# Splitting weights by two transfers on GpSimd's queue, one that rounds and one that accumulates, instead of a load, a cast and a subtraction

## The chip, the cores and the metric

The kernel runs on one core of a Trainium2 chip. The metric is the device time of one execution in microseconds, as the median of several runs. The profile is of one execution; its times are counted from its first instruction.

## What is computed

Two blocks of layers, two layers each, on a sequence of 512 tokens with 1024 features, all in 32-bit floats. The first block has a Fourier mix, windowed attention and attention to a memory in front of a gated feed-forward; the second has a feed-forward, a mixer of three branches and another feed-forward:

```python
for l in range(DEPTH):                       # first block
    h = _rmsnorm(x, g_pre_mix[l]); z = h @ w_in[l]
    y = concat(rmsnorm(fourier), rmsnorm(window attention), rmsnorm(memory attention)) @ w_out[l]
    x = x + _rmsnorm(y, g_post_mix[l])
    gate, up = jnp.split(_rmsnorm(x, g_pre_ffn[l]) @ w_ffn_in[l], 2, axis=-1)
    x = x + _rmsnorm((jax.nn.silu(gate) * up) @ w_ffn_out[l], g_post_ffn[l])
for l in range(DEPTH):                       # second block
    x = x + 0.5 * swiglu(rms_norm(x, ffn1_norm[l]), ffn1_w1[l], ffn1_w2[l])
    x = x + hybrid_mixer(rms_norm(x, mix_norm[l]), ...)   # linear recurrence, attention, depthwise convolution of 31 taps
    x = x + 0.5 * swiglu(rms_norm(x, ffn2_norm[l]), ffn2_w1[l], ffn2_w2[l])
```

## The kernel before

Activations lie with features on the 128 partitions and the 512 tokens along the free dimension, in tiles of 128 x 512 floats ("s", from one pool of 95 slots of 2 KB for each partition). A product of 32-bit floats is made of three matmuls in a shorter float format, fp32r: each operand is split into a rounded part h and a remainder l = value - h, and `mm3` adds wh x al, wl x ah and wh x ah in PSUM. Every weight is used for one pass over the 512 tokens, so all weights stream through once, 12 matmuls for a half tile of 128 x 512 weights.

A weight's way before the change (`wload`, `wsmall`): SP issues a load of up to 1024 columns into "raw" (a pool "wp" of three tiles of 4 KB for each partition); for each half of 512 columns `split` then makes h by a cast (`Plan.copy`, on ScalarE or VectorE) and l by a subtraction (`Plan.tt`, on VectorE or GpSimd), both into slots. Activations are split in the same way, from slots or from PSUM. GpSimd also takes other sums and products of the program through `Plan.tt`, as long as no operand is in PSUM. The only transfers on its queue are the 32 loads of the Fourier tables (`fourier`), from 32-bit floats in HBM into fp32r slots; they round on the way.

The order of all instructions is made ahead by `Plan.schedule`: it simulates the five engines with the prices of `Plan.price`, and among the instructions that are ready and whose tiles find room gives each engine the one that TensorE needs first, up to 120 us ahead of TensorE (AHEAD). An instruction with several possible engines goes to the one that would end it first. The result is a fixed program: each engine works through its own list in order and waits by semaphores. Since every instruction is issued in one helper, `Plan.issue`, all have its line in the profile, L647 before and L646 after the change; groups are told apart by engine, operation and tiles.

In the second block, `mixer` runs `mla` (attention, with the projections of the two other branches as `filler` between), then `dwconv` for four tiles, each a chain of 30 scalar_tensor_tensor instructions on VectorE, one for each tap, with 482 to 511 columns; branches 1 and 0, whose matmuls don't need the convolution; `conv_norm`, which does; and branch 2.

## Time and profile before

| what | value |
|---|---|
| time, median of 3 runs (lowest to highest) | 3626.53 us (3625.71 to 3627.09) |
| span of the profiled execution | 3625.2 us |
| TensorE busy with matmuls | 3460.9 us, 95% |
| VectorE busy | 2558.2 us, 71% |
| ScalarE busy | 1008.3 us, 28% |
| GpSimd busy | 735.2 us, 20% |
| read from HBM | 319.91 MB, 90 GB/s over the span |
| share of the 16 DMA engines | 27.2% for SP's queue, 0.5% for GpSimd's |

Busy time of an engine is the time in which it works on an instruction, and waits inside an instruction count as work. The idle time of an engine is put down to what ended it. The table by stretch (rows 3 below) gives each engine's busy time in that stretch, the number of its instructions in brackets, TensorE's granted clock as a share of full speed, the mean share of the DMA engines and what they moved.

### The profile page before, as it was taken

To read this page: it belongs to the slowest core of one execution; us is meant where nothing else is said; L and a number is where in the kernel's file an instruction comes from. 1 tells how busy PE (TensorE), PEld (TensorE's weight loads), DVE (VectorE), ACT (ScalarE), POOL (GpSimd) and SP (SyncE) were. 2 spreads that over 40 slices of the span, in tenths; PEclk is the share of its full clock that TensorE was granted. 3 is DMA by queue.
4 is the path that set the end of the run, shared out by engine and by line. 5 is a ranking of instruction groups with operands and counts; after the bars stand their busy time and mean duration, and the time that the engine had idled before them with its cause. 6 is when DMAs were issued, how large, how long until landed. Compare 5 with 4: busy or idle time off the path is not lost.

```text
span 3625.2 us, 42725 instructions
## 1 busy us (share of the span) xinstructions
PE 3460.9 (95%) x16280; PEld 2874.0 (79%) x16280; DVE 2558.2 (71%) x4377; ACT 1008.3 (28%) x1944; POOL 735.2 (20%) x582
## 2 busy tenths in 40 slices
PE   7999999989999999999995999999999999599998
PEld 6788888778888888887784888888888878488887
DVE  8987545888553865479999765566556999975553
ACT  5632112453110311037523211021102662321110
POOL 4341003443000400013434000000001243510000
PEclk8999999999999999999997999999999999899999
DMA  4223232232223232331222422332233122242231
GB/s 143 81 66 111 82 102 73 81 99 76 82 94 98 81 109 84 103 118 55 93 72 86 139 76 80 108 121 78 80 112 133 42 72 93 81 138 83 80 104 50
DMA packets 105406, 331.61 MB, mean 91 GB/s; under 512 B 12272, under 2 KB 21232, under 8 KB 105200
## 3 DMA queue, kind: packets, MB, share of 16 engines
q1 hardware_dynamic: 100592, 324.64, 27.2%
q0 software_dynamic: 4608, 4.23, 0.5%
q8 instruction: 128, 2.10, 0.2%
q14 instruction: 78, 0.64, 0.1%
HBM read 319.91 MB, written 6.29 MB: 90 GB/s over the span
## 4 chain that ended last, share of the span: by engine, by line
PE 76%; DVE 21%; issue 2%; ACT 1%; DMA 0%; POOL 0%; SPq 0%; DVEq 0%; ACTq 0%; POOLq 0%
PE ps L647 76%; DVE s L647 20%; ACT s L647 1%; DVE nb L647 0%; DMA s<-in_x 0%; DVE mx L647 0%; DMA raw<-in_a_in 0%; DVE sp L647 0%; POOL rinv L647 0%; SPq L647 0%; DVE rc L647 0%; POOL s L647 0%; DVE sums L647 0%; DVE rms L647 0%; DVEq L647 0%
## 5 line engine op out<-in xcount | busy, mean ns | idle before, releaser
L647 PE MATMUL ps<-s 128*128 128x512 f32 (+3 forms) x15706 | 3399.8, 378 | 44.9 <-DVE s L647 36.0
L647 PEld LDWEIGHTS ps<-s 128*128 128x128 f32 (+1 forms) x15706 | 2804.5, 189 | 609.1 <-DVE s L647 50.0
L647 DVE TENSOR_TENSOR s<-ps,s 128x512 f32<-128x512 f32 (+5 forms) x642 | 394.8, 635 | 515.6 <-PE ps L647 512.2
L647 DVE TENSOR_TENSOR s<-raw,s 128x512 fp32r<-128x512 f32 (+1 forms) x918 | 640.1, 719 | 23.4 <-ACT s L647 5.5
L647 POOL TENSOR_TENSOR s<-s 128x512 f32<-128x512 f32 (+2 forms) x277 | 335.1, 1219 | 1526.6 <-DVE s L647 893.2
L647 POOL TENSOR_TENSOR s<-raw,s 128x512 fp32r<-128x512 f32 (+1 forms) x250 | 366.6, 1480 | 1177.0 <-ACT s L647 534.7
L647 ACT ACTIVATE s<-s 128x512 f32<-128x512 f32 (+1 forms) x325 | 182.6, 579 | 1074.6 <-DVE s L647 1041.1
L647 DVE TENSOR_TENSOR s<-s 128x512 f32<-128x512 f32 (+3 forms) x573 | 423.9, 746 | 60.5 <-ACT s L647 35.9
L647 ACT CAST s<-raw 128x512 fp32r<-128x512 f32 (+1 forms) x564 | 326.4, 606 | 434.9 <-DMA raw<-in_b 181.1
L647 DVE SCALAR_TENSOR_TENSOR s<-s,vecs 128x256 fp32r<-128x256 f32 (+25 forms) x446 | 386.2, 897 | 2.8
L647 DVE CAST s<-raw 128x512 fp32r<-128x512 f32 (+1 forms) x604 | 277.9, 466 | 21.2 <-DMA raw<-in_b 10.9
L647 ACT ACTIVATE s<-s,vecs 128x512 f32<-128x512 f32 (+2 forms) x211 | 134.5, 654 | 389.5 <-DVE s L647 354.2
L647 DVE SCALAR_TENSOR_TENSOR s<-ps,s 128x512 f32<-128x512 f32 (+1 forms) x33 | 22.2, 674 | 236.4 <-PE ps L647 236.4
L647 ACT CAST s<-s 128x512 fp32r<-128x512 f32 (+1 forms) x97 | 58.6, 609 | 235.4 <-DVE s L647 183.2
L647 ACT ACT_TABLE_LOAD x68 | 87.2, 1283 | 54.0 <-DVE s L647 52.2
L647 DVE CAST s<-s 128x512 fp32r<-128x512 f32 (+2 forms) x167 | 87.3, 523 | 14.4 <-POOL s L647 10.6
L647 PE MATMUL ps<-ident,s 128*128 128x128 f32 x392 | 65.9, 293 | 31.0 <-DVE s L647 29.0
L647 ACT ACTIVATE s<-ps 128x512 f32<-128x512 f32 (+1 forms) x40 | 21.3, 533 | 235.6 <-PE ps L647 235.5
L647 DVE RECIPROCAL s<-s 128x128 f32<-128x128 f32 (+1 forms) x48 | 83.3, 1742 | 4.2 <-ACT s L647 4.0
L647 PE MATMUL ps<-s,onesr 128*128 128x512 f32 x36 | 13.0, 444 | 76.5 <-DVE s L647 42.3
L647 PEld LDWEIGHTS ps<-ident,s 128*128 128x128 f32 x392 | 49.3, 149 | 46.2 <-DVE s L647 34.2
L647 ACT ACTIVATE s<-s,nb 128x256 f32<-128x256 f32 (+3 forms) x128 | 70.6, 553 | 37.5 <-DVE nb L647 37.3
(61 smaller groups left out, 701.1 us busy)
## 6 DMA issues: line engine op xcount, KB each, us to landing
raw<-in_b SPq DMA_DIRECT2D x240, 512.0 KB, 3.3
raw<-in_a_f SPq DMA_DIRECT2D x120, 512.0 KB, 3.3
raw<-in_b_in SPq DMA_DIRECT2D x92, 512.0 KB, 3.2
raw<-in_b SPq DMA_DIRECT2D x32, 384.0 KB, 3.6
raw<-in_a_in SPq DMA_DIRECT2D x19, 512.0 KB, 4.2
raw<-in_a_out SPq DMA_DIRECT2D x16, 512.0 KB, 3.2
raw<-in_b_out SPq DMA_DIRECT2D x16, 512.0 KB, 3.2
raw<-in_a_f SPq DMA_DIRECT2D x16, 384.0 KB, 3.6
```

Source lines behind the costliest of these rows:

```text
L647: getattr(getattr(nc, op.eng), op.fn)(*[real(v) for v in op.args], **{k: real(v) for k, v in op.kw.items()})
```

## The change

A half tile of weights no longer passes through "raw". GpSimd's queue issues a transfer from HBM into h that rounds to fp32r; `Plan.scale` makes l = -h (on ScalarE or VectorE); and GpSimd's queue issues a second transfer of the same weights that adds them onto l. Both transfers read the weights from HBM. "wp" is gone, and the pool of slots has 100 instead of 95. `Plan.tt` no longer offers GpSimd. The planner's price for issuing a transfer there is 0.6 instead of 1.0 us, and it now books these transfers on the DMA engines, an accumulating one with double its bytes. The rest of the difference is removed comments.

```diff
     def tt(self, out, in0, in1, op):
-        kw = dict(out=out, in0=in0, in1=in1, op=op)
-        ways = [("vector", "tensor_tensor", (), kw)]
-        if not any(v.tile.psum for v in (out, in0, in1)):
-            ways.append(("gpsimd", "tensor_tensor", (), kw))
-        self.record(ways)
+        self.record([("vector", "tensor_tensor", (), dict(out=out, in0=in0, in1=in1, op=op))])
...
         if fn == "dma_start":
-            return 1.0
+            return 0.6
...
                         elif op.fn == "dma_start":
-                            op.end = now + 4.0
+                            n = int(np.prod(op.kw["out"].shape[1:]))
+                            passes = 2 if "accum_op" in op.kw else 1
+                            state["dma"] = max(state["dma"], now + 1.0) + passes * 128 * n * 4 / 330e3
+                            op.end = state["dma"] + 1.6
...
-    NSLOT = 95
-    RBUFS = 3
+    NSLOT = 100
...
-    def wload(self, src):
+    def halves(self, src):
         nc = self.nc
         n = src.shape[1]
-        raw = nc.tile("wp", "raw", [128, 8, 128], F32, self.RBUFS)[:, :n]
-        for c in (0, 4) if self.fresh else (0,):
-            e = c + 4 if self.fresh else n
-            nc.sync.dma_start(out=raw[:, c:e], in_=src[:, c:e])
-        self.fresh = False
-        hs, ls = [], []
-        for c in range(0, n, 4):
-            e = min(c + 4, n)
-            h, l = (self.t(F32R)[:, :128 * (e - c)].rearrange("p (k c) -> p k c", c=128) for _ in range(2))
-            self.split(raw[:, c:e], h, l)
-            hs.append(h)
-            ls.append(l)
-        return Weights(hs), Weights(ls)
+        h, l = (self.t(F32R)[:, :128 * n].rearrange("p (k c) -> p k c", c=128) for _ in range(2))
+        nc.gpsimd.dma_start(out=h, in_=src)
+        nc.scale(l, h, -1.0)
+        nc.gpsimd.dma_start(out=l, in_=src, accum_op=ALU.add)
+        return h, l
+
+    def wload(self, src):
+        n = src.shape[1]
+        parts = [self.halves(src[:, c:min(c + 4, n)]) for c in range(0, n, 4)]
+        return Weights([h for h, _ in parts]), Weights([l for _, l in parts])
 
     def wsmall(self, src):
-        n = src.shape[1]
-        raw, wh, wl = (self.t(dt)[:, :128 * n].rearrange("p (k c) -> p k c", c=128) for dt in (F32, F32R, F32R))
-        self.nc.sync.dma_start(out=raw, in_=src)
-        self.split(raw, wh, wl)
-        return wh, wl
+        return self.halves(src)
...
-        pools = {k: es.enter_context(tc.tile_pool(name=k, bufs=1)) for k in ("const", "slots", "wp", "sm")}
+        pools = {k: es.enter_context(tc.tile_pool(name=k, bufs=1)) for k in ("const", "slots", "sm")}
```

In the program after the change there are 1196 half tiles (most of 128 x 512, some of 256 or 384 columns) and so 2392 transfers of weights on GpSimd's queue, each of which waits for the completion of the one eight places before it, as transfers on SP's queue do in both programs. The scalings by -1 fall to VectorE 805 times and to ScalarE 391 times.

VectorE in the first mixer of the second block, at the end of the first tile of dwconv (its taps go down to 482 columns); "raw" rows are subtractions for weights, "ps" rows read PSUM. Before:

```order
L647 TENSOR_TENSOR s_16348<-ps_16304,s_14006 128x512
L647 SCALAR_TENSOR_TENSOR s_15970<-s_14364,vecs_115,s_15970 128x484
L647 SCALAR_TENSOR_TENSOR s_16020<-s_14429,vecs_115,s_16020 128x503
L647 TENSOR_TENSOR s_16362<-raw_16287,s_16322 128x512
L647 SCALAR_TENSOR_TENSOR s_15970<-s_14364,vecs_115,s_15970 128x483
L647 TENSOR_TENSOR s_16370<-raw_16287,s_16343 128x512
L647 SCALAR_TENSOR_TENSOR s_15970<-s_14364,vecs_115,s_15970 128x482
```

The same place after:

```order
L646 TENSOR_TENSOR s_16257<-ps_16278,s_16257 128x512
L646 SCALAR_TENSOR_TENSOR s_15978<-s_14376,vecs_109,s_15978 128x484
L646 SCALAR_TENSOR_TENSOR s_15978<-s_14376,vecs_109,s_15978 128x483
L646 SCALAR_TENSOR_TENSOR s_15987<-s_14415,vecs_109,s_15987 128x498
L646 SCALAR_TENSOR_TENSOR s_15978<-s_14376,vecs_109,s_15978 128x482
L646 SCALAR_TENSOR_TENSOR s_15987<-s_14415,vecs_109,s_15987 128x497
```

The subtractions for weights between the taps are gone, and the scalings of the weights that are loaded meanwhile stand on ScalarE's list.

GpSimd in the same mixer, during dwconv. Before:

```order
L647 TENSOR_TENSOR s_16533<-raw_16430,s_16509 128x512
L647 TENSOR_TENSOR s_15911<-s_15911,s_16480 128x512
L647 TENSOR_TENSOR s_16562<-raw_16472,s_16555 128x512
L647 TENSOR_TENSOR s_15964<-s_15964,s_16520 128x512
L647 TENSOR_TENSOR s_16603<-raw_16535,s_16586 128x512
L647 TENSOR_TENSOR s_16649<-s_15970,s_16020 128x512
```

After (s_16274 and s_16312 are remainders, each the second transfer for a half tile):

```order
L646 DMA s_16253<-in_b_lo0 128x512
L646 DMA s_16262<-in_b_in0 128x512
L646 DMA s_16274<-in_b_in0 128x512
L646 DMA s_16295<-in_b_in0 128x512
L646 DMA s_16316<-in_b_in0 128x512
L646 DMA s_16312<-in_b_in0 128x512
```

The subtractions are replaced by transfers, two for each half tile, and the sums that merge the branches (s_15911, s_15964) and that begin conv_norm (s_16649) have gone to VectorE.

GpSimd at the start of the program, after the change, from the 13th transfer on (s_73 and s_101 are the first two rounded halves of the first tile of weights, s_123 and s_186 their remainders):

```order
L646 DMA s_158<-in_a_in0 128x512
L646 DMA s_160<-in_a_in0 128x512
L646 DMA s_166<-in_a_in0 128x512
L646 DMA s_172<-in_a_in0 128x512
L646 DMA s_178<-in_a_in0 128x512
L646 DMA s_182<-in_a_in0 128x512
L646 DMA s_188<-in_a_in0 128x512
L646 DMA s_186<-in_a_in0 128x512
```

The remainder s_123 is the 7th transfer on this list and s_186 the 20th; before, these weights came on SP's list in two of its first eight transfers, between the tiles of x.

## Rows read from the trace of the kernel before

**Rows 1.** The page's first part: busy us, share, instructions of an engine.

```profile
PE 3460.9 (95%) x16280; PEld 2874.0 (79%) x16280; DVE 2558.2 (71%) x4377; ACT 1008.3 (28%) x1944; POOL 735.2 (20%) x582
```

**Rows 2.** What TensorE waited for: us in total, times, longest us.

```profile
PE ps L647 <- DVE s L647: 111.3, 71, 35.3
PE ps L647 <- POOL s L647: 34.2, 1, 34.2
```

**Rows 3.** Stretch: length, PE, PEld, DVE, ACT, POOL busy; PEclk, DMA share, GB/s.

```profile
0.00:243.00 243.00, 208.41 (x1122) 172.88 (x1122) 217.21 (x425) 129.81 (x304) 108.46 (x100) 0.92 0.31 99
243.00:604.00 361.00, 360.71 (x1737) 305.10 (x1738) 207.25 (x345) 65.50 (x124) 44.63 (x40) 1.00 0.28 91
604.00:846.00 242.00, 215.21 (x1277) 179.89 (x1277) 218.19 (x422) 124.87 (x309) 124.22 (x121) 0.96 0.25 79
846.00:1192.00 346.00, 345.74 (x1603) 290.10 (x1602) 188.84 (x318) 47.89 (x84) 27.88 (x22) 1.00 0.28 92
...
1216.00:1605.00 389.00, 389.00 (x1747) 323.19 (x1746) 245.70 (x411) 73.47 (x121) 47.11 (x32) 1.00 0.34 112
1605.00:1964.00 359.00, 312.76 (x1430) 254.12 (x1428) 350.32 (x564) 168.55 (x306) 139.66 (x93) 0.95 0.22 73
1964.00:2800.00 836.00, 835.96 (x3682) 692.32 (x3683) 491.84 (x834) 136.54 (x228) 51.16 (x37) 1.00 0.31 102
...
3168.00:3625.00 457.00, 447.97 (x2041) 373.24 (x2040) 256.80 (x435) 75.66 (x130) 32.20 (x26) 0.99 0.27 90
```

**Rows 4.** VectorE in order of time, second mixer: start us, us, instructions.

```profile
3119.11 4.92 DVE L647 SCALAR_TENSOR_TENSOR s<-s,vecs 128x496 f32<-128x496 f32 x3
...
3124.55 6.25 DVE L647 SCALAR_TENSOR_TENSOR s<-s,vecs 128x493 f32<-128x493 f32 x7
```

**Rows 5.** GpSimd's instructions in order of time at the same place.

```profile
3120.16 3.34 POOL L647 TENSOR_TENSOR s<-raw,s 128x512 fp32r<-128x512 f32 x2
```

**Rows 6.** VectorE from 1605 to 1964: ns min/median/max by tiles; busy, mean ns by group.

```profile
L647 DVE SCALAR_TENSOR_TENSOR s<-s,vecs x146: 650/734/1803, 1614.0 to 1932.6; 128x512 f32<-128x512 f32 x9, 128x511 f32<-128x511 f32 x8, 128x510 f32<-128x510 f32 x8, 128x509 f32<-128x509 f32 x8
L647 DVE TENSOR_TENSOR s<-s x42: 552/688/1771, 1609.6 to 1963.9; 128x512 f32<-128x512 f32 x23, 128x512 fp32r<-128x512 f32 x17, 128x384 fp32r<-128x384 f32 x2
...
L647 DVE SCALAR_TENSOR_TENSOR s<-s,vecs 128x511 f32<-128x511 f32 (+25 forms) x146 | 137.7, 974 | 0.9
L647 DVE TENSOR_TENSOR s<-s 128x512 f32<-128x512 f32 (+2 forms) x42 | 34.4, 833 | 0.8
L647 DVE TENSOR_TENSOR s<-raw,s 128x512 fp32r<-128x512 f32 x30 | 24.4, 824 | 0.0
...
L647 DVE CAST s<-raw x604: 280/419/1527, 14.0 to 3569.8; 128x512 fp32r<-128x512 f32 x143, 128x256 fp32r<-128x256 f32 x8
```

**Rows 7.** GpSimd from 1605 to 1964, by group.

```profile
L647 POOL TENSOR_TENSOR s<-raw,s 128x512 fp32r<-128x512 f32 x68 | 103.0, 1527 | 158.7 <-ACT s L647 95.5 <-issue 27.6 <-PE ps L647 23.3
L647 POOL TENSOR_TENSOR s<-s 128x512 f32<-128x512 f32 (+2 forms) x25 | 37.3, 1496 | 56.9 <-DVE s L647 38.4 <-ACT s L647 18.5
```

**Rows 8.** TensorE at the start, in order of time.

```profile
10.14 22.82 PE L647 MATMUL ps<-s 128*128 128x512 f32 x90 [0.83 <-DVE s L647]
```

**Rows 9.** Packets, MB, share of 16 engines: 5 to 8, 12 to 16, 172.5 to 176 us.

```profile
q1 hardware_dynamic: 480, 0.88, 93.4%
...
q1 hardware_dynamic: 1003, 1.58, 105.4%
...
q0 software_dynamic: 695, 0.65, 85.3%
```

**Rows 10.** The Fourier tables' transfers; VectorE and GpSimd from 761 us on.

```profile
L647 POOL DMA_DIRECT2D s<-in_c_dft x32: 527/567/755, 157.7 to 770.5; - x32
...
DMA to landing us min/median/max: 2.3/2.6/4.2
...
764.69 0.68 DVE L647 TENSOR_TENSOR s<-s 128x512 f32<-128x512 f32 x1
...
761.62 3.76 POOL L647 DMA_DIRECT2D s<-in_c_dft  x7
```

More of the change, by code (lines that the diff above doesn't have):

```diff
@@ L672, in __init__ @@
         self.nl1, self.nl2 = nl1, nl2
-        self.fresh = True
     def t(self, dt=F32):
```

## The prediction

> **What bounds the kernel now.** I read the engines' shares first. TensorE is busy 3460.9 of 3625.2 us, so no change that leaves its work alone can gain more than the 164 us in which it stands; VectorE is busy for 71% of the span, GpSimd for 20% [rows 1]. Next, whom TensorE waits for: VectorE 111.3 us in 71 waits with a longest of 35.3, GpSimd 34.2 us in one wait [rows 2]. Then where: the table by stretch shows two kinds of stage [rows 3]. In five streams (243 to 604, 846 to 1192, 1216 to 1605, 1964 to 2800, 3168 to 3625; 2389 us together) TensorE is busy nearly throughout and the transfers move 90 to 112 GB/s. In the others VectorE is the full engine: it is busy 350.3 of the 359 us of the first mixer of the second block, where TensorE is busy 312.8. Those 46 idle us and as many in the second mixer (the waits of 35.3 and 34.2 us are the ends of dwconv there [rows 2]), and the 61 idle us of the two stages of the first block in the table are what can be had.
>
> Last, why VectorE is full there. Three taps of dwconv that run beside GpSimd's arithmetic take 4.92 us, seven that mostly do not take 6.25 [rows 4]; two of GpSimd's subtractions lie over the slow ones, 1.67 us each, as long as a slow tap (1.64) [rows 5]. So VectorE's instructions with two operands in SBUF wait for GpSimd's. Over the mixer this shows as a mean of 974 ns against a median of 734 for the taps (146 of them) and 833 against 688 for the products and sums (42) [rows 6].
>
> **The change part by part.** The new kernel has 1196 half tiles of weights (256 KB as a rule). Each loses a load on SP's queue, a cast and a subtraction, and gets two transfers on GpSimd's queue with a scaling by -1 between them.
>
> *The subtractions go.* VectorE loses 24.4 us of them in the mixer [rows 6], GpSimd 68 of 1527 ns [rows 7]. The cast becomes a scaling of the same size on the same engines: VectorE's casts of weights have a median of 419 ns [rows 6], and I take the same for the scaling, so it costs nothing in the mixer, where the order puts about as many on VectorE as before and the rest on ScalarE, which is idle half of the time [rows 3]. Over the whole program VectorE gets 805 scalings where it had 604 casts of raw tiles; the 200 more are 84 us, in the streams, where it is busy about 60% of the time.
>
> *GpSimd's other arithmetic moves to VectorE.* In the mixer that is 25 instructions [rows 7] at VectorE's undisturbed 688 ns, 17.2 us. Against it the waiting of VectorE goes: 146 x 240 ns = 35.0 us and 42 x 145 ns = 6.1 us [rows 6]. VectorE's sum in the mixer is 350.3 - 24.4 - 35.0 - 6.1 + 17.2 = 302 us, below TensorE's 312.8. TensorE is then the bound there, and of 46 idle us I take 40, leaving 6 for the short chain in conv_norm; twice, since both mixers read alike: **-80 us**. In the two stages of the first block [rows 3] VectorE is as full, but gets more of GpSimd's sums there, and the waits are those of short chains; I take 15 of 61 idle us, bounds 0 and 30: **-15 us**.
>
> *The start.* Before, the last 90 of the first 96 matmuls ended at 33 us [rows 8]. Now the remainder of the second half tile is the 20th transfer on GpSimd's queue (by the order shown with the change), behind 19 others and beside the 8 loads of x on SP: at 0.9 us and 0.66 us each (below) that is 22 us, and some 80 of the matmuls, 17 us, come after it. They end at about 41: **+8 us**, bounds 0 and 15.
>
> *The transfers.* This decides. A half tile was 256 KB once, now it is 256 KB rounded and 256 KB accumulated. The streams move 234.7 MB as read from their rows, 895 half tiles of 0.262 MB in 2389 us, so TensorE asks for one every **2.67 us** [rows 3]. What a pair takes on the 16 engines, the trace brackets only.
> - Rounding: plain loads with rows of 2 KB ran at 0.88 MB in 3 us at a share of 93.4%, 314 GB/s, 0.84 us for a half tile; under a full queue 1.58 MB went in 4 us, 0.66 us. The one transfer of this kind that exists, the Fourier tables, of 1 KB rows, ran at 0.65 MB in 3.5 us at 85.3%, 218 GB/s, 1.20 us [rows 9]. Bounds 0.66 and 1.20; I take 0.95, because half as many rows for the bytes save part of the difference.
> - Accumulating: no row. Lower bound a plain copy, 0.66; upper bound twice the Fourier tables' rate, 2.40, if the read of the destination costs as much as that of the source. I take 1.5, near two plain reads (1.33 to 1.67).
> The pair is 2.45 us (bounds 1.32 and 3.60), 92% of 2.67: it is hidden, **0 us**. In the hungriest stream, 112 GB/s or 2.34 us for each of 166, it may cost up to 18 us, which the slots filled ahead should carry. Cover gone, every 0.1 us over 2.67 costs 90 us.
>
> For the accumulating transfer there is a rule. The Trainium skill (Collectives: The Full Stack, The bandwidth ceiling: the fold count and why AG ≠ RS ≠ AR) says that a summing transfer reads two sources through one ring and so runs at about half of a copy, measured ratio 1.93. By that, an estimate from its ratio, the pair would be 0.95 + 1.93 x 0.84 = 2.57 us, still hidden but with no margin; no row here shows an accumulating transfer.
>
> *Issuing.* GpSimd's queue gets 2392 more transfers. The 32 there take 567 ns each in the median [rows 10], so 1356 us of 3625, and 1.13 of 2.67 us for each half tile: hidden. They do not hold VectorE up as the arithmetic did: beside seven of them a VectorE sum with SBUF operands took 0.68 us [rows 10]. Each accumulating one waits for its scaling, and all later loads queue behind it; it also waits for the transfer 8 before it, so a transfer may take 8 x 1.33 = 10.7 us to land, against 2.6 for the Fourier tables [rows 10]. SP's queue is left with x, the rope swaps and masks, which no longer queue behind weights: no charge.
>
> **Sum.** 3625.2 - 80 - 15 + 8 = 3538 us of the profiled span; the timed runs' median is 1.3 above it, so **3540 us**, -2.4%.
>
> **The rivals.**
> *The transfers become the bound.* It decides from a pair of 2.67 us on, and eats the gain of 87 us at 2.77. Its price, with the rounding at the Fourier tables' rate and the second read at the plain rate (1.20 + 1.20 + 0.66 = 3.06 us): 895 x 0.39 = 350 us, 3890 us, slower. At the upper bound of 3.60 it is 4370. For it: that the only rounding transfers here are slower than plain ones, and the sum of my own choices lies only 8% below the need. Against it: these rows are short, and DMA engines stand idle for 72% of a stream now. TensorE would then wait for DMA all through the streams and VectorE's relief would not count.
> *GpSimd's queue blocks.* An accumulating transfer whose scaling stands behind a gate's sigmoid or a PSUM read keeps all later loads back. In the streams 1.5 us per half tile are free; at the some dozen entries of stages, 5 us each would be 60 us: 3600 us, still faster. Against it: before, SP's queue waited for the same engines and TensorE hardly noticed.
> *VectorE does not come free,* because issuing on GpSimd holds it like arithmetic. Then the 80 us stay, 3620 us, no change. The row beside the seven issues speaks against it.
>
> **How the numbers follow.** Forecast 0.60, transfers as the bound 0.33, blocked queue 0.04, VectorE not freed 0.03. A measurement can tell about 0.2% (7 us) from no change. Faster: 0.60 + 0.04 and nothing of the others, 0.64. Same: 0.03 and a sliver of the pair times around 2.77, 0.04. Slower: 0.32. The range goes down to 3480 (all 92 idle us of the mixers and 53 of the first block's, no loss at the start) and up to 3930, a pair of 3.1 us, which leaves about 0.13 above and 0.04 below. Since both signs hold much, the forecast's own range is 3490 to 3600.
>
> **What would show it.** Right: in the streams TensorE is busy 99% as before, with DMA shares of 80 to 95%; VectorE's taps have a mean near 734 ns; the waits of 35 us at the end of dwconv are gone; the first 96 matmuls end near 41 us. Wrong: TensorE's waits name DMA, accumulating transfers land after 8 us or more with all 8 in flight, and the streams are longer by the same factor; or GpSimd's issues take 1 us and more and its queue never empties.

## The result, and the profile after

The changed kernel takes 3527.1 us (median of 4 runs, 3525.06 to 3528.27) against 3626.8 for the kernel before on the same chips: a ratio of 0.9725, 95% interval 0.9712 to 0.9739. It is faster by 100 us; 3540 had been predicted. The profiled execution has a span of 3525.2 us.

The page's first part and the transfers of GpSimd's queue (packets, MB, share of the 16 DMA engines' span); then whom TensorE waited for (us in total, times, longest us):

```profile
PE 3446.0 (98%) x16280; PEld 2869.9 (81%) x16280; DVE 1941.6 (55%) x3942; ACT 882.9 (25%) x1709; POOL 1756.8 (50%) x2447
...
q0 software_dynamic: 349056, 616.75, 81.8%
...
PE ps L646 <- DVE s L646: 44.1, 32, 8.0
PE ps L646 <- DMA s<-in_c_chan: 13.3, 1, 13.3
PE ps L646 <- ACT s L646: 7.3, 8, 4.1
PE ps L646 <- DMA s<-in_a_mv: 2.1, 1, 2.1
...
PE ps L646 <- DMA s<-in_a_in: 1.3, 2, 1.1
```

Against [rows 1, 2] TensorE stands 79 us instead of 164, the two waits of some 35 us are gone, and DMAs are named for the first time, in four waits of 16.7 us together, 13.3 of them in the one at the start. VectorE has lost 617 us of busy time. The table by stretch, with the columns of [rows 3], from the first block's first stage to the first mixer:

```profile
0.00:250.00 250.00, 208.78 (x1119) 171.36 (x1120) 182.11 (x438) 120.78 (x285) 104.57 (x152) 0.94 0.71 166
250.00:611.00 361.00, 361.00 (x1741) 305.26 (x1740) 148.91 (x309) 50.05 (x98) 178.78 (x248) 1.00 0.82 173
611.00:849.00 238.00, 215.49 (x1276) 183.68 (x1275) 182.07 (x458) 117.64 (x295) 100.04 (x143) 0.91 0.68 151
...
1213.00:1602.00 389.00, 387.43 (x1749) 321.77 (x1748) 167.65 (x328) 53.08 (x86) 221.23 (x307) 1.00 0.95 208
1602.00:1910.00 308.00, 306.22 (x1428) 252.17 (x1427) 292.06 (x560) 168.09 (x303) 146.01 (x202) 1.00 0.79 166
```

TensorE runs through the streams as before, at DMA shares of 82 to 95%. The mixer has shrunk from 359 to 308 us; VectorE works 292 us in it instead of 350, and TensorE 306 instead of 313, at a granted clock of 1.00 instead of 0.95. Before, the clock was granted at the lower of its two levels (1.2 instead of 2.4 GHz) from 1905.7 to 1939.9 us, beginning inside the 35 us in which TensorE stood:

```profile
1936.39 1.22 PE L647 MATMUL ps<-s,onesr 128*128 128x512 f32 x2 [35.26 <-DVE s L647]
```

No such wait and no stretch at the lower level is left in the mixer. VectorE's groups there after the change (busy us, mean ns), to be held against [rows 6]:

```profile
L646 DVE SCALAR_TENSOR_TENSOR s<-s,vecs 128x511 f32<-128x511 f32 (+29 forms) x146 | 101.1, 732 | 2.6 <-ACT s L646 1.5
...
L646 DVE TENSOR_TENSOR s<-s 128x512 f32<-128x512 f32 (+1 forms) x66 | 43.7, 684 | 0.7
```

The taps have a mean of 732 ns instead of 974, about the median that they had before.

**Prices of the transfers.** What moved from 38.5 to 45 us, in 40 equal slices, while eight transfers were queued. Up to the 26th slice (42.7 us) these are accumulating transfers, the last of which land at 40.99, 42.26, 43.57 and 44.84 us, then three rounding ones, which land at 45.53, 46.18 and 46.83 us:

```profile
GB/s 202 202 202 202 202 202 214 202 214 189 202 202 202 227 214 202 189 202 214 202 202 227 202 214 189 227 366 479 340 353 366 378 378 366 366 391 378 353 265 252
```

An accumulating transfer moves its 0.262 MB at some 205 GB/s, 1.28 us; a rounding one at some 370, 0.7 us. Over all streams, the intervals between landings in a full queue have a median of 0.67 us for rounding and 1.28 or 1.29 us for accumulating transfers (1132 whole half tiles of each in the program). So a pair takes 1.96 us of the engines. What TensorE asks for in this kernel, counted by landings, is one half tile in 2.60 us in the hungriest stream (1213 to 1602) and in 2.74 to 3.13 us in the others, 2.86 on the mean; more of the weights than before are loaded ahead of the streams.

For the comparisons, the table gives the lengths of four stages in us, each counted between the same matmuls of TensorE in every kernel (1122, 1275, 1428 and 1486 of them), and the median time of the whole. The names are those of the experiments below.

| kernel | first block, first stage | first block, second stage | first mixer | second mixer | whole |
|---|---|---|---|---|---|
| before | 243.3 | 242.0 | 358.6 | 367.9 | 3626.5 |
| after | 250.5 | 238.2 | 308.4 | 322.6 | 3527.1 |
| before_vec | 226.9 | 227.3 | 349.9 | 362.6 | 3572.8 |
| gp_back | 262.1 | 250.1 | 336.4 | 351.1 | 3622.4 |
| idle_sums | 252.4 | 241.3 | 326.6 | 337.8 | 3569.2 |
| plain_second | 245.4 | 234.0 | 307.8 | 320.9 | 3514.8 |
| fold30 | 252.2 | 238.0 | 308.8 | 321.6 | 3527.8 |
| plan_late | 239.0 | 225.6 | 309.1 | 321.3 | 3499.8 |
| block1_loads | 228.6 | 220.0 | 309.2 | 321.8 | 3485.0 |
| mix_late | 223.7 | 221.0 | 309.3 | 321.2 | 3479.9 |

### The profile page after: what moved, and what is told of

Same layout as the page of the kernel before. It is cut to its first block, busy times and chain, and to the rows that moved or that the text cites. A ratio compares the mean times of both kernels' runs of the same rounds, so it can differ in the third digit from the quotient of the medians.

```text
span 3525.2 us, 44631 instructions
## 1 busy us (share of the span) xinstructions
PE 3446.0 (98%) x16280; PEld 2869.9 (81%) x16280; DVE 1941.6 (55%) x3942; ACT 882.9 (25%) x1709; POOL 1756.8 (50%) x2447
## 3 DMA queue, kind: packets, MB, share of 16 engines
q0 software_dynamic: 349056, 616.75, 81.8%
## 4 chain that ended last, share of the span: by engine, by line
PE 91%; DVE 4%; DMA 2%; issue 2%; ACT 0%; POOL 0%; SPq 0%; POOLq 0%; DVEq 0%; ACTq 0%
PE ps L646 91%; DVE s L646 4%; DMA s<-in_b_in 1%; ACT s L646 0%; POOL s L646 0%; DMA s<-in_a_in 0%; DMA s<-in_c_chan 0%; DMA s<-in_x 0%; DVE mx L646 0%; POOL rinv L646 0%; DVE sp L646 0%; SPq L646 0%; DVE rc L646 0%; DVE nb L646 0%; DVE sums L646 0%
## 5 line engine op out<-in xcount | busy, mean ns | idle before, releaser
L646 PE MATMUL ps<-s 128*128 128x512 f32 (+2 forms) x15706 | 3381.5, 376 | 45.2 <-DVE s L646 26.2
L646 POOL DMA_DIRECT2D s<-in_b x1088 | 786.3, 1028 | 667.9 <-DVE s L646 296.6
L646 ACT ACTIVATE s<-s 128x512 fp32r<-128x512 f32 (+3 forms) x716 | 404.6, 601 | 1737.5 <-DVE s L646 1128.4
L646 DVE TENSOR_TENSOR s<-ps,s 128x512 f32<-128x512 f32 (+4 forms) x642 | 397.8, 636 | 637.5 <-PE ps L646 631.8
L646 DVE TENSOR_SCALAR s<-s 128x512 fp32r<-128x512 f32 (+2 forms) x845 | 341.3, 423 | 471.5 <-DMA s<-in_b 278.5
L646 POOL DMA_DIRECT2D s<-in_a_f x544 | 396.9, 1082 | 348.4 <-DVE s L646 163.2
L646 DVE TENSOR_TENSOR s<-s 128x512 f32<-128x512 f32 (+2 forms) x822 | 500.3, 624 | 54.8 <-ACT s L646 33.3
L646 POOL DMA_DIRECT2D s<-in_b_in x368 | 287.8, 1008 | 266.7 <-ACT s L646 88.7
L646 DVE SCALAR_TENSOR_TENSOR s<-s,vecs 128x256 fp32r<-128x256 f32 (+25 forms) x446 | 287.9, 678 | 6.3 <-ACT s L646 3.2
L646 DVE SCALAR_TENSOR_TENSOR s<-ps,s 128x512 f32<-128x512 f32 (+1 forms) x33 | 22.2, 674 | 183.0 <-PE ps L646 183.0
L646 DVE CAST s<-s 128x512 fp32r<-128x512 f32 (+1 forms) x190 | 81.9, 431 | 6.8 <-DMA s<-in_pos 1.2
L646 POOL DMA_DIRECT2D s<-in_a_in x80 | 58.8, 884 | 24.9 <-DMA s<-in_a_in 13.1
```

The costliest lines, as they stand in the source:

```text
L646: getattr(getattr(nc, op.eng), op.fn)(*[real(v) for v in op.args], **{k: real(v) for k, v in op.kw.items()})
```

## The experiments

### One part alone: no arithmetic on GpSimd, weights still loaded

```diff
--- before
+++ before_vec
-        if not any(v.tile.psum for v in (out, in0, in1)):
-            ways.append(("gpsimd", "tensor_tensor", (), kw))
         self.record(ways)
```

> The kernel before with sums and products offered to VectorE alone: GpSimd does no elementwise arithmetic, but the weights still come by load, cast and subtraction, now all on VectorE. Theory 1 (VectorE waits for GpSimd's arithmetic; that goes, 35.0 + 6.1 us in a mixer, but 68 subtractions and 25 sums at 0.69 us come, 64 us): VectorE's sum in a mixer 350 - 41 + 64 = 373 us, so each mixer is some 15 to 25 us longer than before, the whole 3655 to 3680 us, the taps' mean near 735 ns. Rival 2 (the taps were slow for another reason, no waiting goes): 350 + 64 = 414 us in a mixer, the whole 3730 us and more, the taps' mean near 970 ns.

It took 3572.8 us, 0.9852 of before (0.9835 to 0.9868): 54 us faster, where both theories had it slower. The page's first part, the first mixer's row, and VectorE's groups in it:

```profile
PE 3457.2 (97%) x16280; PEld 2871.9 (80%) x16280; DVE 2500.7 (70%) x4788; ACT 1060.5 (30%) x2056; POOL 37.2 (1%) x55
...
1567.00:1917.00 350.00, 315.19 (x1430) 256.78 (x1429) 338.69 (x641) 171.37 (x314) 1.49 (x1) 0.95 0.20 66
...
L645 DVE SCALAR_TENSOR_TENSOR s<-s,vecs 128x511 f32<-128x511 f32 (+26 forms) x146 | 100.6, 733 | 0.7
...
L645 DVE TENSOR_TENSOR s<-raw,s 128x512 fp32r<-128x512 f32 x87 | 57.5, 685 | 0.1
L645 DVE TENSOR_TENSOR s<-s 128x512 f32<-128x512 f32 (+2 forms) x72 | 47.1, 682 | 0.6
```

The taps' mean of 733 ns is theory 1's. But VectorE's sum in the mixer is 339 us, not 373: with 77 more instructions than before it is busy 12 us less. The sums and subtractions are busy 46 us more than before (104.6 against 58.8), where 58 had been reckoned (64, less 6.1 of waiting). And the waiting was larger than the two groups of [rows 6] that the estimate had used: the subtractions too went from a mean of 824 to 685 ns, the casts from slot to slot from 725 to 424. Over the whole program GpSimd has 527 instructions fewer (55 against 582 [rows 1]), VectorE 411 more and ScalarE 112 more, taken here for copies that left VectorE. By an estimate at 0.68 us for a sum and 0.42 for a copy VectorE has 527 x 0.68 - 112 x 0.42 = 311 us more work, and it is busy 57 us less: 368 us of waiting have gone with some 700 us of arithmetic on GpSimd, half of it. The first block's two stages gain 16 and 15 us by this line alone.

### The other part alone: transfers, with arithmetic on GpSimd

```diff
--- after
+++ gp_back
-        self.record([("vector", "tensor_tensor", (), dict(out=out, in0=in0, in1=in1, op=op))])
+        kw = dict(out=out, in0=in0, in1=in1, op=op)
+        ways = [("vector", "tensor_tensor", (), kw)]
+        if not any(v.tile.psum for v in (out, in0, in1)):
+            ways.append(("gpsimd", "tensor_tensor", (), kw))
+        self.record(ways)
```

> The changed kernel with GpSimd offered to the planner again for sums and products without a PSUM operand; weights still come by the two transfers. GpSimd gets 209 such instructions, some 25 in each mixer, 24 and 31 in the two stages of the first block, the rest in the streams. Theory 1 (what filled VectorE in the mixers were 93 instructions of GpSimd there, and the weights' 68 subtractions are most of them): 25 instructions of 1.5 us cost VectorE 25/93 of the 41 us of waiting, 11 us, and take 25 x 0.69 = 17 us off it, so the mixers stay within 5 us; the whole 3520 to 3545 us against 3527. Rival 2 (any arithmetic on GpSimd gives part of the gain back, in proportion): 25/93 of the 95 us gained in the mixers, 3553 us and more, with the taps' mean over 800 ns (732 without it).

It took 3622.4 us, 0.9988 of before (0.9979 to 0.9998). 209 instructions on GpSimd give back 95 of the 100 us, more than three times what rival 2 had, and theory 1 falls. In the first mixer 22 of them run. The lines show the mixer's row, VectorE's taps there, GpSimd's sums, and then VectorE and GpSimd in order of time where the mixer's last chain passes:

```profile
1640.00:1976.00 336.00, 311.59 (x1428) 254.70 (x1427) 302.94 (x552) 164.62 (x298) 177.19 (x223) 0.97 0.75 155
...
L650 DVE SCALAR_TENSOR_TENSOR s<-s,vecs 128x511 f32<-128x511 f32 (+25 forms) x146 | 114.0, 819 | 4.8 <-ACT s L650 3.9
...
L650 POOL TENSOR_TENSOR s<-s 128x512 f32<-128x512 f32 (+1 forms) x22 | 37.5, 1715 | 13.7 <-DVE s L650 12.0 <-PE ps L650 0.8 <-ACT s L650 0.7
...
1943.61 1.49 DVE L650 TENSOR_TENSOR s<-s 128x512 f32<-128x512 f32 x2 [0.16 <-ACT s L650]
1955.57 0.69 DVE L650 TENSOR_TENSOR s<-s 128x512 f32<-128x512 f32 x1 [10.47 <-ACT s L650]
...
1949.02 0.53 POOL L650 DMA_DIRECT2D s<-in_b_co  x1 [0.51 <-DMA s<-in_b_in]
1950.88 0.53 POOL L650 DMA_DIRECT2D s<-in_b_out  x1 [1.33 <-DMA s<-in_b_co]
1953.05 0.53 POOL L650 DMA_DIRECT2D s<-in_b_out  x1 [1.65 <-issue]
1953.60 1.27 POOL L650 TENSOR_TENSOR s<-s 128x512 f32<-128x512 f32 x1
```

Two things are to be seen. The taps are slow again, 819 ns. And GpSimd's sum at 1953.60 is the subtraction of the mean from the fourth tile in conv_norm; VectorE had done that for the other three tiles by 1945.1. The fourth stood in GpSimd's list behind transfers, each of which waits for the completion of an earlier one ("DMA s<-in_b_in" as the releaser). VectorE then idles 10.47 us until ScalarE's square of that tile, and TensorE 15.9. The next run shows the first of the two alone.

### GpSimd's arithmetic without anyone waiting for it

```diff
--- after
+++ idle_sums
...
             getattr(getattr(nc, op.eng), op.fn)(*[real(v) for v in op.args], **kw)
+            if op.eng == "gpsimd" and op.fn == "dma_start":
+                n += 1
+                if n % 9 == 0:
+                    nc.gpsimd.tensor_tensor(out=self.idle, in0=self.idle, in1=self.idle, op=ALU.add)
...
```

> The changed kernel in the same order with a sum of 128x512 that nobody reads on GpSimd after every ninth transfer, 265 in all and some 22 in each mixer, as many as GpSimd's sums there in the kernel with both transfers and arithmetic on GpSimd, which lost 28 us in each mixer. Nothing waits for these sums. Theory 1 (VectorE waits for GpSimd's arithmetic while it lasts, 0.45 us for each us of it by the totals of the two pairs of kernels): 22 x 1.7 x 0.45 = 17 us in each mixer, 5 to 10 in each of the two stages of the first block, nothing in the streams, 3570 to 3590 us, the taps' mean near 800 ns. Rival 2 (the loss came from sums that stood behind held-up transfers in GpSimd's queue, with VectorE waiting for their results): 3527 to 3540 us.

It took 3569.2 us, 0.9845 of before (0.9828 to 0.9861): 42 us more than the changed kernel, and 1 below theory 1's range. The mixers are longer by 18.2 and 15.2 us, theory 1's 17; the first block's stages by 1.9 and 3.1, less than it said; VectorE is not full there (182 of 250 and of 238 us). The page's first part; VectorE's taps and the idle sums in the first mixer (1612 to 1938.5 us), and these sums in the whole program:

```profile
PE 3455.7 (97%) x16280; PEld 2873.4 (81%) x16280; DVE 2108.3 (59%) x3942; ACT 884.3 (25%) x1709; POOL 2058.0 (58%) x2717
...
L648 DVE SCALAR_TENSOR_TENSOR s<-s,vecs 128x511 f32<-128x511 f32 (+29 forms) x146 | 112.7, 813 | 2.7 <-ACT s L648 1.6
...
L652 POOL TENSOR_TENSOR idle<-idle 128x512 f32<-128x512 f32 x23 | 39.4, 1713 | 0.0
...
L652 POOL TENSOR_TENSOR idle<-idle 128x512 f32<-128x512 f32 x269 | 440.2, 1636 | 0.6
```

VectorE has the same 3942 instructions as in the changed kernel and is busy 166.7 us longer, for 269 sums that take 440 us: 0.38 us of waiting for each us of GpSimd's arithmetic over the whole program. In the first mixer it is more: VectorE is busy some 314 us there instead of 292, for 39.4 us of sums. The Trainium skill (SBUF — State Buffer, SBUF: two separate sides) says that a VectorE instruction with two inputs in SBUF and a GpSimd instruction that reads SBUF exclude one another for their whole length; the taps' 732 ns without such sums and 813 beside them agree. So rival 2 does not hold alone: sums for which nobody waits cost 42 us. How the 28 us that gp_back lost in each mixer divide does not follow from this run, since gp_back also took 22 sums off VectorE. By gp_back's own row VectorE is busy 11 us longer than in the changed kernel, in spite of the sums that it no longer has, and idle 33 us instead of 16; 10.5 of these 17 are the wait behind GpSimd's queue. How the 12 us divide that gp_back lost in each of the first block's stages was not measured.

### The price of accumulating, and how near the transfers are to the end

```diff
--- after
+++ plain_second
-            getattr(getattr(nc, op.eng), op.fn)(*[real(v) for v in op.args],
-                                                **{k: real(v) for k, v in op.kw.items()})
+            kw = {k: real(v) for k, v in op.kw.items() if k != "accum_op"}
+            getattr(getattr(nc, op.eng), op.fn)(*[real(v) for v in op.args], **kw)
```

> The changed kernel in the same order, but the second transfer does not accumulate: it copies the rounded part again over the scaled tile, so the remainders are wrong and the output isn't the reference's. It gives the price of accumulating. In the changed kernel's first 45 us, with eight transfers queued, a rounding one lands 0.67 us after the last, an accumulating one 1.29 us. Theory 1 (these intervals are the price, a pair is 1.96 us of the 2.67 that TensorE takes for a half tile, hidden): the second transfers land at 0.67 us intervals too, the streams stay as they are, the share of the DMA engines in them falls by a third or so, and only the start may gain, 0 to 8 us: 3519 to 3529 us. Rival 2 (the transfers are at their limit, as a share of 82 to 95% in the streams says): the streams come out shorter or the small idle times of TensorE go, 3515 us and less.

It took 3514.8 us, 0.9693 of before (0.9679 to 0.9707), 12 us less than the changed kernel. That is 4 below what theory 1 allowed and just within rival 2's number, but not by its mechanism: the first stream takes 361 us as before, and 9 of the 12 us come in the first block's two stages. The second transfers land at intervals of 0.67 us. GpSimd's queue and its largest group of issues, of the changed kernel and then of this one (mean ns behind the busy us):

```profile
L646 POOL DMA_DIRECT2D s<-in_b x1088 | 786.3, 1028 | 667.9 <-DVE s L646 296.6
```

```profile
q0 software_dynamic: 349056, 616.75, 62.5%
...
L647 POOL DMA_DIRECT2D s<-in_b x1088 | 586.8, 557 | 860.4 <-DVE s L647 502.9
```

The same bytes take the engines 62.5% instead of 81.8% of the span, and an issue takes 557 ns, as the Fourier tables' did [rows 10], instead of 1028. It is the accumulating transfer whose issue is long, 0.84 us and more in the first 40 us of the changed kernel, and some rounding ones behind it are longer too (1.05 and 1.27 us, against 0.53 to 0.58 beside their own kind).

A third transfer for each half tile, first on GpSimd's queue:

```diff
--- after
+++ third
...
             getattr(getattr(nc, op.eng), op.fn)(*[real(v) for v in op.args], **kw)
+            if "accum_op" in kw:
+                nc.gpsimd.dma_start(out=self.junk[n % 16][:, :kw["in_"].shape[1]], in_=kw["in_"])
+                n += 1
...
```

> The changed kernel in the same order with a third transfer after each accumulating one: the same 256 KB from HBM, copied to a scratch tensor in HBM that nobody reads. Theory 1 (a pair takes 1.96 us, a third copy 0.67): 2.63 us for a half tile against 2.67 wanted on the mean; only the two hungriest streams are over it, 166 half tiles x 0.29 (2.34 wanted) and 325 x 0.06 (2.57 wanted), 67 us, less what the slots filled ahead carry: 3540 to 3600 us, with TensorE waiting for DMA there and nowhere else. Rival 2 (the share of busy DMA engines is the true load, so a pair takes about 2.45 us): 3.1 us and more for a half tile, 0.45 x 895 = 400 us, 3930 us. Rival 3 (issuing on GpSimd is the limit: 1.0 us for each transfer): 3.0 us for a half tile, 0.33 x 895 = 300 us, 3830 us, with no idle time on GpSimd in the streams.

It took 3903.7 us (1.077 of before, 1.0753 to 1.0786). The number is rival 2's, the mechanism is not: transfers still land after one another at 0.67, 1.28 and 0.67 us in a full queue, 2.6 us for a half tile. By the changed kernel's landings that is enough for every stream but the hungriest, which asks for just as much. Yet the first stream, which asks for one half tile in 3.03 us there, needs 397 us instead of 361. Its row, then whom TensorE waited for in the whole program:

```profile
273.00:670.00 397.00, 373.63 (x1740) 309.18 (x1739) 147.40 (x305) 50.48 (x98) 247.45 (x370) 0.98 0.96 236
...
PE ps L648 <- DVE s L648: 230.4, 63, 18.6
PE ps L648 <- DMA s<-in_b: 32.9, 24, 4.7
```

Rival 3 falls too: GpSimd is busy 247 of these 397 us. In the first stream TensorE waits in short pieces for DMA (22.2 us in 16 waits), and it is busy 12.6 us longer at a granted clock of 0.98 instead of 1.00. Over the program most of its waiting is for VectorE. The longest of these waits, TensorE and then VectorE in order of time:

```profile
1288.59 3.62 PE L648 MATMUL ps<-s 128*128 128x256 f32 x28 [0.56 <-DMA s<-in_a_f]
1310.77 1.02 PE L648 MATMUL ps<-ones,s 128*128 128x1 f32 x4 [18.57 <-DVE s L648]
...
1299.05 0.43 DVE L648 TENSOR_SCALAR s<-s 128x512 fp32r<-128x512 f32 x1 [3.75 <-DMA s<-in_b]
1305.98 0.43 DVE L648 TENSOR_SCALAR s<-s 128x512 fp32r<-128x512 f32 x1 [6.50 <-DMA s<-in_b]
1308.51 0.43 DVE L648 TENSOR_SCALAR s<-s 128x512 fp32r<-128x512 f32 x1 [2.10 <-DMA s<-in_b]
1308.85 0.74 DVE L648 TENSOR_SCALAR s<-ps,vecs 128x512 f32<-128x512 f32 x1
1309.51 1.21 DVE L648 TENSOR_TENSOR s<-s 128x512 f32<-128x512 f32 x2
```

TensorE needs the sums at 1309.51, which read what it had finished at 1292. On VectorE's list scalings of the second block's weights (in_b) stand in front of them, and each waits for its rounded part to land. So late transfers of weights for the next block hold up the activations of this one. Of the 230 us for VectorE, VectorE itself stood before such a scaling for 64; how much of the rest goes back to landings by longer ways was not followed.

Two further forms take the causes apart, on SP's queue, and with 8 columns on GpSimd's:

```diff
--- third
+++ third_sp
...
-                nc.gpsimd.dma_start(out=self.junk[n % 16][:, :kw["in_"].shape[1]], in_=kw["in_"])
+                h = real(self.first_part[op.kw["out"].tile]).bitcast(F32)
+                nc.sync.dma_start(out=self.junk[n % 16][:, :h.shape[1]], in_=h)
...
```

> The changed kernel in the same order with a third transfer for each half tile, on SP's queue this time: it copies the rounded part from SBUF to a scratch tensor in HBM once it is there. The third transfer on GpSimd's queue cost 377 us although transfers still landed 0.67, 1.28 and 0.67 us after one another, 2.6 us for a half tile. Theory 1 (the 16 engines are the limit: at 2.6 of 2.67 us the queue is never full when it should be): 3850 us and more again. Rival 2 (GpSimd's queue is: eight transfers in flight make 2.7 half tiles instead of 4, and issues follow one another in order): 3530 to 3600 us.

```diff
--- third
+++ third_tiny
-                nc.gpsimd.dma_start(out=self.junk[n % 16][:, :kw["in_"].shape[1]], in_=kw["in_"])
+                nc.gpsimd.dma_start(out=self.junk[n % 16][:, 0, :8], in_=kw["in_"][:, 0, :8])
```

> The changed kernel in the same order with a third transfer on GpSimd's queue after each accumulating one, but of 8 columns, 4 KB in 128 rows: it costs GpSimd an issue and one of the eight places in flight and moves next to nothing. Theory 1 (the 16 engines were the limit of the third transfer): 3527 to 3560 us. Rival 2 (issues or the eight places were): 3700 us and more, with GpSimd's queue never idle for long in the streams.

On SP's queue the third transfer costs 215 us (3742.5; 1.0322 of before, 1.0301 to 1.0342), on GpSimd's queue without bytes 81 us (3608.0; 0.995, 0.9935 to 0.9966). Neither theory of the two has it alone: the load on the engines is the larger part, places and issues on GpSimd's queue the smaller, and the 377 us of both together are more than their sum. The form on SP's queue also differs from the first in its source, SBUF instead of HBM, so the division is rough. On SP the five streams grew by 8, 21, 42, 51 and 5 us, the two mixers by 55 together and the first block's two stages by 31, though by the landings of the changed kernel the mean need reaches 2.6 us in the third stream alone. TensorE begins to wait before the mean load reaches the mean need. The scalings that stand on VectorE's and ScalarE's lists ahead of activations are one way to this, seen above. No run moved them, and that the transfers also come in bursts, whenever slots come free, was not tried either.

### The start, and the first block

```diff
--- after
+++ fold30
         wf = self.t()[:, :128 * n]
+        nc.lead = 30.0
         nc.sync.dma_start(out=wf, in_=I["a_four"])
         ch = self.t()[:, :256]
         nc.sync.dma_start(out=ch, in_=I["c_chan"])
+        nc.lead = nc.AHEAD
```

> The changed kernel with one thing moved: the loads of the Fourier weights and the channel table (a_four, c_chan) are planned at most 30 us ahead of TensorE's need instead of 120, so that their 16 matmuls no longer stand at the head of TensorE's list, where TensorE waits 13.3 us for c_chan. Theory 1 (that wait is the start's loss): the first 96 matmuls of the projections end at 45 us instead of 50, and 3520 to 3524 us. Rival 2 (the remainder of the second half tile, landed at 27 us, and the later waits for VectorE set the stage's end): the wait moves to that remainder and later stages of the chain, 3525 to 3529 us.

It took 3527.8 us (0.9726 of before, 0.971 to 0.9742), no change: rival 2. TensorE at the start, first in the changed kernel, then here:

```profile
8.00 0.79 PE L646 MATMUL ps<-s 128*128 128x512 f32 x1 [8.00 <-DVE s L646]
22.09 9.06 PE L646 MATMUL ps<-s 128*128 128x64 f32 x31 [13.30 <-DMA s<-in_c_chan]
...
31.45 18.53 PE L646 MATMUL ps<-s 128*128 128x512 f32 x81
```

```profile
15.98 5.67 PE L646 MATMUL ps<-s 128*128 128x512 f32 x14 [2.35 <-DMA s<-in_a_in]
30.35 20.28 PE L646 MATMUL ps<-s 128*128 128x512 f32 x80 [8.70 <-DMA s<-in_a_in]
```

The wait for the channel table only stood in front of the wait for the second half tile's remainder, which here lands at 30.2 us. The first 96 matmuls of the projections end at 49.3 us in the one and 50.4 in the other.

```diff
--- after
+++ block1_loads
     def halves(self, src):
         h, l = (self.t(F32R)[:, :128 * n].rearrange("p (k c) -> p k c", c=128) for _ in range(2))
+        if self.loads:
+            raw = self.t()[:, :128 * n].rearrange("p (k c) -> p k c", c=128)
+            nc.sync.dma_start(out=raw, in_=src)
+            self.split(raw, h, l)
+            return h, l
         nc.gpsimd.dma_start(out=h, in_=src)
```

`loads` is True while the first block is recorded, False for the second.

> The changed kernel with the first block's weights split as before (a load on SP's queue into a slot, a cast, a subtraction, this one on VectorE); the second block's weights stay with the two transfers, and GpSimd does no elementwise arithmetic. By stages, the kernel before with all sums on VectorE was 24 us shorter than the changed one in the first stage of the first block and 11 in the second, 41 and 40 longer in the two mixers, and equal in the streams. Theory (each stage keeps its own cost): 3527 - 34 = 3492 us, range 3485 to 3502. Rival (the first block is slow for the other slots or orders of the changed kernel, not for the transfers): 3515 us and more.

It took 3485.0 us, 0.9611 of before (0.9596 to 0.9625), at the lower end of the theory's range. Each stage keeps its own cost, so the transfers are worth 41 us in a mixer (before_vec against this one, which also differ in slots and order) and cost 22 and 18 us in the first block's stages (the changed kernel against this one).

```diff
--- after
+++ plan_late (and, from block1_loads, mix_late)
-                            passes = 2 if "accum_op" in op.kw else 1
-                            state["dma"] = max(state["dma"], now + 1.0) + passes * 128 * n * 4 / 330e3
-                            op.end = state["dma"] + 1.6
+                            passes = 1.92 if "accum_op" in op.kw else 1
+                            state["dma"] = max(state["dma"], now + 1.0) + passes * 128 * n * 4 / 390e3
+                            op.end = state["dma"] + 4.2
```

> The changed kernel with the planner told what was measured: a rounding transfer takes the engines 0.67 us and an accumulating one 1.29 (before 0.79 and 1.59), and both land 5.9 us after their issue when nothing is queued (before 3.4). Theory 1 (the first block is 34 us slower than with loads because scalings by -1 stand on VectorE's and ScalarE's lists before their rounded part has landed, and the attention's short chains stand behind them): the first block's two stages get 10 to 25 us shorter, 3502 to 3517 us in all, and ScalarE's waits for DMA of 14.0 and 5.0 us there go. Rival 2 (a half tile's way of two landings is simply too long for stages where loads are asked for late): 3522 to 3535 us.

It took 3499.8 us, 0.9653 of before (0.9638 to 0.9667), 2 us below theory 1's range. The first block's stages are 11.5 and 12.6 us shorter, as it said. ScalarE's waits for these weights in the changed kernel, first stage and then second:

```profile
ACT s L646 <- DMA s<-in_a_out: 14.0, 1, 14.0
...
ACT s L646 <- DMA s<-in_a_out: 7.8, 3, 5.0
```

With the new prices the first stage has none, the second this one:

```profile
ACT s L646 <- DMA s<-in_a_out: 4.8, 1, 4.8
```

A scaling that stands on ScalarE's list before its rounded part has landed holds up what stands behind it, and with the measured time of landing the wait of 14.0 us is gone; the one of 5.0 us is not. The whole order is new with these prices, so that all of the 24 us come from such waits is argued, not shown. The start stays as it was (the 96 matmuls end at 50.1 us). Against the loads of the next run, whose planner has the same prices, 15 and 5 us of the first block's 22 and 18 remain: rival 2 has a part too.

> The kernel with loads in the first block and the two transfers in the second, with the same measured prices for transfers in the planner. TensorE stood 52 of 3486 us there, a few of them in the mixers. Theory 1 (late landings still cost the second block): 3475 to 3482 us. Rival 2 (the second block has nothing left to lose to them): 3483 to 3490 us.

It took 3479.9 us, 0.9596 of before (0.958 to 0.9612), and is the fastest kernel here: 147 us below before and 47 below the changed one. The time is theory 1's, but the gain of 5 us on block1_loads is smaller than the spread of that kernel's four runs (3480.6 to 3488.1). Its place fits only in part: of the 7.8 us between the two profiled spans 4.9 lie in the first block's first stage, where only the Fourier tables are on GpSimd's queue, and 3.2 in the stream ahead of the first mixer. The page's first part:

```profile
PE 3433.8 (99%) x16280; PEld 2859.7 (82%) x16280; DVE 2079.2 (60%) x4137; ACT 966.6 (28%) x1871; POOL 1240.5 (36%) x1727
```

## Why the prediction was right, point by point

- **The bound**, right. The 46 idle us in the first mixer and 43 in the second came from VectorE, and 2 are left in each.
- **The mixers**, right in kind, 15 us too small: 80 was said, 50.2 and 45.3 came. VectorE's sum was put at 302 us and is 292; the taps at 734 ns, measured 732. One term was missing: TensorE's own busy time fell from 313 to 306 us in the first mixer and from 325 to 321 in the second, with a granted clock of 1.00 instead of 0.95.
- **What the mixers' gain rests on**, half right. The prediction charged VectorE's waiting to two groups, 41 us a mixer. The runs give 0.38 to 0.53 us of waiting for each us of GpSimd's arithmetic over the whole program, which reaches other groups too (subtractions and casts, above). And neither part of the change gives the gain alone: the one line in tt gives 54 us, the transfers with arithmetic left on GpSimd 4, both 100. The five more slots and the planner's new prices were not run by themselves. That a sum on GpSimd would queue behind transfers was not seen; the rival of the blocked queue spoke of loads only.
- **The first block's stages and the start** share the first stage, so the two terms are best taken together: -15 and +8 were said, -7 us for the two stages, and +7.2 and -3.8 came, +3.4. Another -6 came in the two pieces behind the second stage. What was missed is that the transfers cost 11 us in the second stage (against before_vec), where they land some 6 us after their issue and the planner reckoned 3.4.
- **The start by itself** came by another way: the first 96 matmuls end at 49 us, not 41, 16 us later than before and not 8. The working added up engine time (22 us until the second remainder) and left out that it lands 5.5 us after its issue, which itself waits for a place among eight. Later waits then lay under it: before, TensorE waited another 8.84 us for VectorE at 54 us, and no such wait follows here until 92 us. That the stage came out 7.2 us longer, near the +8, is luck.
- **The transfers**, right that they are hidden; the price was 2.45 us and is 1.96. The rounding was sized from the Fourier tables, 0.95, and takes 0.67, the plain copy's lower bound. The short rows were not to blame: in a full queue the changed kernel's rounding transfers of 128 KB in rows of 1 KB land 0.34 us apart in the median, the same rate. The Fourier tables had been issued 0.54 us apart (seven in 3.76 us [rows 10]), so the queue was not full, and the share of 85.3% by which their rate was divided overstates the load. Accumulating was 1.5 and is 1.28. The Trainium skill's rule (Collectives: The Full Stack, The bandwidth ceiling: the fold count and why AG ≠ RS ≠ AR) of 1.93 copies for a sum of two sources, which that page measured between ranks, agrees with the measured 1.28 / 0.67 = 1.91; the prediction applied it to a copy of 0.84 us.
- **The edge**, wrong. "Every 0.1 us over 2.67 costs 90 us" makes the need a sharp limit. With 2.6 us the kernel already lost 377 us, or 215 where GpSimd's queue did not carry the third transfer. So the chance of 0.33 for this rival was not too large, and that the forecast of no cost held is in part luck: it held at 1.96 us, and whether it would have held at the 2.45 us that were forecast was not tried.
- **Issuing**, 567 ns was said, 1028 came, for the accumulating transfers' sake; issues overlap, so GpSimd is busy 1757 us, half of the span. Issues of 1 us and more with a queue that never empties had been named as a sign of being wrong; the first came, the second did not. That issuing does not hold VectorE up is right: with 1196 more issues (third_tiny) VectorE is busy 1943.8 us instead of 1941.6.

## What to carry to other kernels

Where VectorE is full, arithmetic that GpSimd takes off it comes back as waiting, here 0.38 to 0.53 us for each us of it, so count both engines before sharing work between them. A queue that carries many transfers should carry nothing that a short chain waits for, and an engine's list should have nothing that waits for a landing in front of what TensorE needs next. A planner therefore has to know when a transfer lands, not only what it takes of the engines. Choose the way of loading by stage: two transfers are cheap where VectorE is full (a mixer gains 41 us), and a load with a cast and a subtraction was better in the first block's stages, where chains are short and VectorE has room (182 of 250 us busy in the first).

## What was not expected of the hardware

- A transfer that rounds to fp32r costs the DMA engines the same as a plain one, 0.67 us for 256 KB in rows of 2 KB; one that accumulates onto SBUF 1.28 us, and its issue on GpSimd's queue 0.84 us and more instead of 0.53.
- The share of busy DMA engines overstates the load: 82% in the first stream, where 119 half tiles at 1.96 us make 65% of 361 us, and 62% with plain second transfers, where 1.34 us make 44%. The intervals between landings in a full queue are the better price.
- At 2.6 us of transfers for a mean need of 2.86 the kernel takes 11% longer (third); where between 1.96 and 2.6 the loss begins was not measured.
